# The delta rule's state stepped with the inverse multiplied out

## The chip, the cores and the metric

One core of a Trainium2 chip runs the whole program. The metric is device microseconds of one execution; the median of three runs of the kernel before is 2524.68 us. Engines: PE (TensorE matmul), DVE (VectorE), ACT (ScalarE), POOL (GpSimd), SP (SyncE, which issues most DMAs).

## The reference

A trunk of two layers on 256 tokens of width 2048. Layer 0 mixes by windowed attention and by a bidirectional gated delta rule, layer 1 by a Fourier transform; both have a SwiGLU network behind. The change concerns the delta rule of layer 0. For each of 8 heads and two directions it steps a 128x128 state `s` through the chunks, first those of the context, then those of the sequence:

```
sol = lax.linalg.triangular_solve(jnp.eye(DELTA_CHUNK, dtype=jnp.float32) + m, rhs, ...)
u, w = sol[..., :dv], sol[..., dv:]

def step(s, xs):
    u_i, w_i, attn_i, q_i, k_i, gl_i = xs
    v_new = u_i - jnp.einsum('bhcd,bhde->bhce', w_i, s)
    o_i = jnp.einsum('bhcd,bhde->bhce', q_i, s) + jnp.einsum('bhcs,bhse->bhce', attn_i, v_new)
    s = s * jnp.exp(gl_i)[..., None, None] + jnp.einsum('bhcd,bhce->bhde', k_i, v_new)
    return s, o_i
```

Everything is float32. With the inverse of the triangular matrix called Z, `v_new` is Z times (values minus scaled keys times state); it can be had as Z times that difference, or as Z times values minus (Z times scaled keys) times state.

## The kernel before

The kernel takes chunks of 128 tokens, so there are 4 chunks (2 of the context, 2 of the sequence), and 4 groups `g` of 2 heads. With 2 directions that gives 4 chains `q` to a group, and one PSUM tile of 128x512 holds a set of four 128x128 products, one a chain.

Work is written as Python generators. `gdn_a(g)` makes decays, the matrices and 16x16 blocks of the inverse (L729, L731 on DVE, with round trips through DRAM, `dz` and `dy`); `gdn_b(g)` completes the inverse `Z` and steps the state. Both are added to a list behind the projections of group `g`, and `step()` runs a piece of each whose time has come. That time is a count of PE work kept while the program is written (`clock`): after `yield 2` a piece waits for 2 x 1.2 us of counted matmul time, which the projections (tiles `acc`, three float32r products of split weights `whi`, `wlo`) fill. The tile framework then orders each engine's queue and sets the waits; every engine runs its queue in that order.

A step `t` of the chain (L845 to L899) before: keys times state into `pks` (PE); values plus scaled `pks` into `r` (tile `rw`, L854, DVE, four instructions); Z times `r` into `pw` (PE); `pw` scaled into `dv` (L865, ACT, four) and, where an output is due, `pw` as it is into `w` (L868, ACT, one wide); keys times `dv` into `pS` (PE); the state `St` from itself and `pS` (L883, or copies at L881 in the first step, DVE, four). In the last two steps query times state and attention times `w` make the output (L893 to L897). A `yield 2` parts the sets of products.

Beside the chain run, on DVE, the dots of `ada_dot` (L274, tile `araw`), each on 512 KB that SP loads; on ACT and POOL the splitting of weights (L197, L203); then attention (its probabilities in tiles `C2`, L1016, three buffers) and, at L1085, the gated output.

Of the kernel before, what the change touches and what calls it, by code (L numbers as in the profile page):

```python
# [11 lines left out]
F32R = mybir.dt.float32r  # L12
BF16 = mybir.dt.bfloat16
AF = mybir.ActivationFunctionType
ALU = mybir.AluOpType
AX = mybir.AxisListType

P = 128
# [7 lines left out]
HD = 128  # L26
# [45 lines left out]
def trunk(ctx: ExitStack, tc: tile.TileContext, a: dict, dbg=None, stop=None):  # L72
# [10 lines left out]
    def T(shape, tag, bufs, dt=F32):  # L83
        uid[0] += 1
        return sb.tile(list(shape), dt, tag=tag, bufs=bufs, name=f"{tag}_{uid[0]}")

    def C(shape, name, dt=F32):
        return sb.tile(list(shape), dt, tag=name, bufs=1, name=name)
# [10 lines left out]
    def ktok(shape, dt=F32):  # L99
        return T(shape, "KTOK", 1, dt)  # L100

    def vtok(shape, dt=F32):
        return T(shape, "VTOK", 1, dt)
# [7 lines left out]
    def qch(shape, dt=F32):  # L111
        return T(shape, "QCH", 2, dt)

    def e2(shape, dt=F32):
        return T(shape, "E2", 3, dt)
# [8 lines left out]
    def sm():  # L124
        uid[0] += 1
        return ps.tile([P, 512], F32, tag="sm", bufs=4, name=f"sm_{uid[0]}")
# [3 lines left out]
    def mm(out, l, r, start, stop):  # L130
        clock[0] += max(64, int(np.prod(r.shape[1:]))) * (4 if r.dtype == F32 else 1) / 2400.0
        nc.tensor.matmul(out, l, r, start=start, stop=stop)  # L132
# [4 lines left out]
    V = nc.vector  # L137
    S = nc.scalar
# [331 lines left out]
    for c in range(4):  # L470
# [3 lines left out]
                    in1=smallr[:, 0:1, :].to_broadcast([P, 4, 16]), op=ALU.add)  # L474
# [10 lines left out]
                           in1=ea.unsqueeze(1).to_broadcast([P, 4, 16]), op0=ALU.mult, op1=ALU.mult)  # L485
# [4 lines left out]
    egl = C([P, 4, 8, 2], "egl")  # L490
    pgc = sm()
    for d in range(2):
# [7 lines left out]
                           in1=gc.rearrange("p c h d -> p c (h d)"), op0=ALU.mult, op1=ALU.subtract)  # L500
# [121 lines left out]
    def bl(i, n=32):  # L622
        return slice(n * i, n * i + n)
# [118 lines left out]
    def gdn_b(g):  # L742
# [3 lines left out]
        K, Q, Z, Zv, A, Zc = (H[n] for n in ("K", "Q", "Z", "Zv", "A", "Zc"))  # L746
        ner, dvs, so1, so2 = H["sc"]
# [4 lines left out]
        if g == 0:  # L752
            Kt, Vt = H["Kt"], H["Vt"]
        else:
            Kt, Vt = ktok([P, 2, 4, HD]), vtok([P, 2, 4, HD])
# [86 lines left out]
        seqs = [(0, 1, 2, 3), (1, 0, 3, 2)]  # L842
        chains = [(hh * 2 + d, hh, d) for hh in range(2) for d in range(2)]
        St = T([P, 4, HD], "St", 1)
        for t in range(4):  # L845
            if t > 0:
                r = T([P, 4, HD], "rw", 2)
                pks = sm()
                for q, hh, d in chains:
                    c = seqs[d][t]  # L850
                    mm(pks[:, bl(q, P)], K[:, hh, bl(c, P)], St[:, q], True, True)
                for q, hh, d in chains:
                    c = seqs[d][t]
                    V.scalar_tensor_tensor(out=r[:, q], in0=pks[:, bl(q, P)], scalar=ner[:, c, hh, d:d + 1],  # L854
                                           in1=Vt[:, hh, c], op0=ALU.mult, op1=ALU.add)
                yield 2
            pw = sm()
            for q, hh, d in chains:
                c = seqs[d][t]
                mm(pw[:, bl(q, P)], Z[d][:, c, hh, :], r[:, q] if t > 0 else Vt[:, hh, c], True, True)  # L860
            if t < 3:
                dv = T([P, 4, HD], "rw", 2)
                for q, hh, d in chains:
                    c = seqs[d][t]
                    S.activation(dv[:, q], pw[:, bl(q, P)], AF.Copy, scale=dvs[:, c, hh, d:d + 1])  # L865
            if t >= 2:
                w = e2([P, 4, HD])
                S.activation(w.rearrange("p q f -> p (q f)"), pw, AF.Copy)  # L868
            yield 2
            if t >= 2:  # L870
                pqs = sm()
                for q, hh, d in chains:
                    mm(pqs[:, bl(q, P)], Q[:, hh, bl(seqs[d][t] - 2, P)], St[:, q], True, True)
            if t < 3:
                pS = sm()
                for q, hh, d in chains:
                    mm(pS[:, bl(q, P)], Kt[:, hh, seqs[d][t]], dv[:, q], True, True)
                for q, hh, d in chains:
                    c = seqs[d][t]
                    if t == 0:  # L880
                        V.tensor_copy(St[:, q], pS[:, bl(q, P)])  # L881
                    else:
                        V.scalar_tensor_tensor(out=St[:, q], in0=St[:, q], scalar=egl[:, c, 2 * g + hh, d:d + 1],  # L883
                                               in1=pS[:, bl(q, P)], op0=ALU.mult, op1=ALU.add)
            if t >= 2:
                paw = sm()
                for q, hh, d in chains:
                    mm(paw[:, bl(q, P)], A[:, d, hh, seqs[d][t] - 2], w[:, q], True, True)
                for q, hh, d in chains:
                    c = seqs[d][t] - 2  # L890
                    o = ogdn[c][:, 2 * g + hh]
                    if t == 2:
                        S.activation(o, pqs[:, bl(q, P)], AF.Copy, scale=so1[:, c, hh, d:d + 1])  # L893
                    else:
                        V.scalar_tensor_tensor(out=o, in0=pqs[:, bl(q, P)], scalar=so1[:, c, hh, d:d + 1], in1=o,
                                               op0=ALU.mult, op1=ALU.add)
                    V.scalar_tensor_tensor(out=o, in0=paw[:, bl(q, P)], scalar=so2[:, c, hh:hh + 1], in1=o,  # L897
                                           op0=ALU.mult, op1=ALU.add)
            yield 2  # L899


    def proj(warr, npair, lhs, tiles, kept=None, nkeep=0, last=0):
# [170 lines left out]
    for hf in range(2):  # L1073
# [9 lines left out]
        for t in range(2):  # L1083
            for h in range(4):
                V.scalar_tensor_tensor(out=zs[:, t, h], in0=ogdn[t][:, hf * 4 + h], scalar=rz[:, t * 4 + h:t * 4 + h + 1],  # L1085
                                       in1=zs[:, t, h], op0=ALU.mult, op1=ALU.mult)
        for hp in range(2):
            p = sm()
# [204 lines left out]
    for l in range(2):  # L1293
        if l == 1:
            plan_out(lambda n: a["w_four"][n], 8, NKF, 8)
        for j in range(NJ):
            for i in range(2):
                w = [a["w_gu"][l, j, i, q] for q in range(8)]
# [11 lines left out]
    def load_dft():  # L1310
        while f"hid{NJ - 2}" not in done:
            yield 1
        raws = [qch([P, 516]), qch([P, 512]), T([P, 512], "Zc", 1)]
        for i, src in enumerate((a["k_dft_d"], a["k_dft_l"][:, 0], a["k_dft_l"][:, 1])):
            nc.sync.dma_start(raws[i], src.rearrange("p k n -> p (k n)"))
        while f"hid{NJ - 1}" not in done:
            yield 1
        for f in (lambda: T([P, 516], "C2", 3, F32R), lambda: e2([P, 512], F32R), lambda: T([P, 512], "rw", 2, F32R)):
            dft.extend([f(), f()])
        for i in range(3):  # L1320
            yield DY
            split(dft[2 * i], dft[2 * i + 1], raws[i])
        yield DY
        dft.extend([c2([P, 512], F32R), T([P, 512], "Y64", 1, F32R)])
        for i in range(2):
            V.tensor_scalar_mul(dft[6 + i], dft[4 + i].bitcast(F32), -1.0)
# [191 lines left out]
```

## Time and profile before

| | |
|---|---|
| median of 3 runs | 2524.68 us (2523.31 to 2525.12) |
| the profiled execution | 2527.05 us |
| its span | 2525.2 us |
| first state step of group 0 on PE | 358.83 us |
| last state update of group 3 on DVE | 757.3 us |

The span runs from the first instruction to the last; the execution's time has 1.85 us around it. Terms of a sum are made against the profiled execution, which lies 2.37 us above the median of the runs. In rows of the trace a product of four chains shows as x8, two rows to each float32 product; x2 in the names of a queue's order counts equal rows in a row.

### The profile page before, as it was taken

What the parts mean: (1) busy time and instruction counts of PE and PEld (TensorE: products, weight loads), DVE (VectorE), ACT (ScalarE), POOL (GpSimd) and SP (SyncE); (2) the same over time, 40 slices, a digit from 0 to 9 for tenths busy, and PEclk for the clock granted to TensorE, in tenths of its full rate; (3) what the DMA queues carried; (4) which work ended last, traced back from release to release, by engine and by line L of the source; (5) the groups of instructions that cost most, each with busy time, mean ns of one, the idle gap of its engine ahead of it and who ended that gap; (6) DMA issues with size and microseconds to landing.
All of it is one profiled execution on the core that took longest, in us unless ns stands there. A gap on an engine that the chain in (4) does not pass through costs nothing.

```text
span 2525.2 us, 39613 instructions
## 1 busy us (share of the span) xinstructions
PE 2388.6 (95%) x14520; PEld 2022.8 (80%) x14520; DVE 1775.6 (70%) x3204; ACT 1274.6 (50%) x2298; POOL 332.5 (13%) x286
## 2 busy tenths in 40 slices
PE   7999888978799999999999999899999999999997
PEld 7998678867677788888888887697788888888886
DVE  4678788778657777877778788747666665555556
ACT  3337433544465654554445454646654554445455
POOL 1214434245431100000000000101100000000001
PEclk7999989989899999999999999999999999999998
DMA  6675778677837569999898998636577777666665
GB/s 252 244 288 197 236 224 272 208 245 253 263 130 237 197 228 316 312 312 317 319 318 312 315 322 308 211 102 217 191 235 242 232 237 234 193 191 189 191 201 191
DMA packets 218483, 611.04 MB, mean 242 GB/s; under 512 B 68905, under 2 KB 69913, under 8 KB 217521
## 3 DMA queue, kind: packets, MB, share of 16 engines
q1 hardware_dynamic: 168016, 581.59, 68.7%
q10 hardware_dynamic: 46528, 15.21, 2.6%
q0 software_dynamic: 3744, 11.71, 1.4%
q8 instruction: 114, 1.87, 0.3%
q14 instruction: 81, 0.66, 0.1%
HBM read 595.03 MB, written 13.40 MB: 241 GB/s over the span
## 4 chain that ended last, share of the span: by engine, by line
PE 70%; DVE 10%; DMA 6%; issue 3%; ACT 2%; POOL 1%; SPq 0%; ACTq 0%; DVEq 0%; POOLq 0%
PE acc L132 65%; PE sm L132 4%; DMA araw<-in_ada_d 4%; DVE araw L274 3%; DVE S L1153 1%; PE sm L1236 1%; DVE wlo L203 1%; POOL wlo L203 1%; ACT whi L197 1%; DVE C L513 1%; DVE T L729 0%; DMA T<-dy 0%; DVE T L731 0%; DMA T<-dz 0%; DMA raw<-in_w_dn 0%
## 5 line engine op out<-in xcount | busy, mean ns | idle before, releaser
L197 ACT ACTIVATE whi<-raw 128x512 fp32r<-128x512 f32 (+1 forms) x1306 | 817.9, 630 | 858.4 <-DVE wlo L203 489.1
L203 DVE TENSOR_TENSOR wlo<-raw,whi 128x512 fp32r<-128x512 f32 x1140 | 788.7, 699 | 469.8 <-ACT whi L197 468.1
L132 PE MATMUL acc<-whi,S 128*128 128x512 f32 x3312 | 1047.1, 394 | 8.1 <-ACT whi L197 3.7
L132 PEld LDWEIGHTS acc<-whi,S 128*128 128x128 f32 x3312 | 626.7, 190 | 139.5 <-ACT whi L197 4.5
L132 PE MATMUL acc<-wlo,S 128*128 128x512 f32 x1656 | 651.0, 393 | 3.8 <-DVE wlo L203 1.9
L274 DVE SCALAR_TENSOR_TENSOR araw<-araw,cb 128x1024 f32<-128x1024 f32 x320 | 415.6, 1300 | 66.9 <-DMA araw<-in_ada_d 66.3
L132 PEld LDWEIGHTS acc<-wlo,S 128*128 128x128 f32 x1656 | 314.1, 190 | 69.0 <-POOL wlo L203 2.9
L203 POOL TENSOR_TENSOR wlo<-raw,whi 128x512 fp32r<-128x512 f32 x166 | 245.7, 1493 | 445.2 <-ACT whi L197 429.3
L132 PE MATMUL acc<-S,whi 128*128 128x256 f32 x1152 | 235.1, 296 | 5.1 <-ACT whi L197 3.4
L132 PEld LDWEIGHTS acc<-S,whi 128*128 128x128 f32 x1152 | 193.3, 201 | 5.8 <-ACT whi L197 3.6
L132 PE MATMUL acc<-S,wlo 128*128 128x256 f32 x576 | 169.7, 296 | 2.0 <-POOL wlo L203 2.0
L1113 POOL DMA_DIRECT2D drow<-K x4 | 2.0, 508 | 1273.9 <-DVE K L1111 1273.9
L132 PE MATMUL acc<-whi,ZT 128*128 128x512 f32 x384 | 122.1, 392 | 0.0
L132 PEld LDWEIGHTS acc<-S,wlo 128*128 128x128 f32 x576 | 115.9, 201 | 3.5 <-POOL wlo L203 2.6
L132 PE MATMUL acc<-whi,KCH 128*128 128x512 f32 x320 | 110.7, 402 | 1.1 <-ACT whi L197 1.1
L132 PE MATMUL acc<-whi,A 128*128 128x512 f32 x312 | 106.0, 395 | 0.0
L132 PE MATMUL acc<-whi,T 128*128 128x512 f32 x296 | 99.5, 392 | 0.0
L132 PEld LDWEIGHTS acc<-whi,ZT 128*128 128x128 f32 x384 | 72.1, 188 | 15.3
L132 PE MATMUL acc<-wlo,KCH 128*128 128x512 f32 x192 | 78.0, 406 | 4.3 <-DVE wlo L203 4.1
L132 PE MATMUL acc<-wlo,ZT 128*128 128x512 f32 x192 | 75.6, 394 | 0.2 <-POOL wlo L203 0.2
L132 PEld LDWEIGHTS acc<-whi,KCH 128*128 128x128 f32 x320 | 62.2, 195 | 15.2 <-ACT whi L197 1.5
L132 PE MATMUL acc<-wlo,T 128*128 128x512 f32 x176 | 68.8, 391 | 0.0
(437 smaller groups left out, 2829.2 us busy)
## 6 DMA issues: line engine op xcount, KB each, us to landing
raw<-in_w_gu SPq DMA_DIRECT2D x347, 512.0 KB, 4.4
araw<-in_ada_d SPq DMA_DIRECT2D x320, 512.0 KB, 4.8
raw<-in_w_dn SPq DMA_DIRECT2D x179, 512.0 KB, 4.4
raw<-in_w_att SPq DMA_DIRECT2D x40, 512.0 KB, 4.4
raw<-in_w_gdn SPq DMA_DIRECT2D x34, 512.0 KB, 4.8
raw<-in_w_out SPq DMA_DIRECT2D x30, 512.0 KB, 3.7
ZT<-in_ada_s SPq DMA_DIRECT2D x24, 512.0 KB, 3.7
raw<-in_w_four SPq DMA_DIRECT2D x21, 512.0 KB, 3.7
```

What stands on the lines that cost most here:

```text
L132: nc.tensor.matmul(out, l, r, start=start, stop=stop)
L197: S.activation(hi[:, :w], raw[:, c:c + w], AF.Copy)
L203: eng.tensor_sub(lo[:, :w], raw[:, c:c + w], hi[:, :w].bitcast(F32))
L274: V.scalar_tensor_tensor(out=junk, in0=w, scalar=1.0, in1=rows, op0=ALU.mult, op1=ALU.mult, accum_out=dst)
L513: V.scalar_tensor_tensor(out=ca[:, :, lo:hi], in0=pv[:, :, lo + o:hi + o], scalar=wconv[:, blk, j:j + 1], in1=ca[:, :, lo:hi], op0=ALU.mul ...
L1113: nc.gpsimd.dma_start(drow.rearrange("h k p -> (h k) p"), gt)
L1153: V.scalar_tensor_tensor(out=x[:, t, sl], in0=y[:, t, sl], scalar=r, in1=x[:, t, sl], op0=ALU.mult, op1=ALU.add)
L1236: nc.tensor.transpose(p[:, i * P:(i + 1) * P], hv[t][:, i * P:(i + 1) * P], ident)
```

## The change

The step is taken apart differently. `weights(t + 1)`, a step ahead, scales the keys (L854 of the new file, ACT, four, tile `C2`), multiplies them by Z (PE) and copies the product to `wt` (L864, DVE, one wide copy into `rw`). Z times values then goes to `pw`, and `wt` times state is added to it in the accumulator. `pw` is evacuated once, wide (L878, ACT); the scale that was on `dv` goes on a second scaled copy of the keys, `kd` (ACT, four, `C2`), which also is made ahead. The first state is one wide copy (L891); L894 answers to L883. The pauses are 1.5 in place of 2, two of them a step, `rw` has three buffers in place of two, and the evacuated `w` lives there and no longer in `E2`.

```diff
--- before.py
+++ after.py
@@ -842,31 +842,43 @@
         seqs = [(0, 1, 2, 3), (1, 0, 3, 2)]
         chains = [(hh * 2 + d, hh, d) for hh in range(2) for d in range(2)]
         St = T([P, 4, HD], "St", 1)
+
+        def flat(v):
+            return v.rearrange("p q f -> p (q f)")
+
+        def scaled(tag, by, t):
+
+            kk = T([P, 4, HD], tag, 3)
+            for q, hh, d in chains:
+                c = seqs[d][t]
+                S.activation(kk[:, q], Kt[:, hh, c], AF.Copy, scale=by[:, c, hh, d:d + 1])
+            return kk
+
+        def weights(t):
+
+            kn = scaled("C2", ner, t)
+            p = sm()
+            for q, hh, d in chains:
+                mm(p[:, bl(q, P)], kn[:, q], Z[d][:, seqs[d][t], hh, :], True, True)
+            wt = T([P, 4, HD], "rw", 3)
+            V.tensor_copy(flat(wt), p)
+            return wt
+
+        kd = scaled("C2", dvs, 0)
+        wt = None
         for t in range(4):
-            if t > 0:
-                r = T([P, 4, HD], "rw", 2)
-                pks = sm()
-                for q, hh, d in chains:
-                    c = seqs[d][t]
-                    mm(pks[:, bl(q, P)], K[:, hh, bl(c, P)], St[:, q], True, True)
-                for q, hh, d in chains:
-                    c = seqs[d][t]
-                    V.scalar_tensor_tensor(out=r[:, q], in0=pks[:, bl(q, P)], scalar=ner[:, c, hh, d:d + 1],
-                                           in1=Vt[:, hh, c], op0=ALU.mult, op1=ALU.add)
-                yield 2
             pw = sm()
             for q, hh, d in chains:
-                c = seqs[d][t]
-                mm(pw[:, bl(q, P)], Z[d][:, c, hh, :], r[:, q] if t > 0 else Vt[:, hh, c], True, True)
+                mm(pw[:, bl(q, P)], Z[d][:, seqs[d][t], hh, :], Vt[:, hh, seqs[d][t]], q == 0, t == 0 and q == 3)
+            if t > 0:
+                yield 1.5
+                for q, hh, d in chains:
+                    mm(pw[:, bl(q, P)], wt[:, q], St[:, q], False, q == 3)
+            w = T([P, 4, HD], "rw", 3)
+            S.activation(flat(w), pw, AF.Copy)
             if t < 3:
-                dv = T([P, 4, HD], "rw", 2)
-                for q, hh, d in chains:
-                    c = seqs[d][t]
-                    S.activation(dv[:, q], pw[:, bl(q, P)], AF.Copy, scale=dvs[:, c, hh, d:d + 1])
-            if t >= 2:
-                w = e2([P, 4, HD])
-                S.activation(w.rearrange("p q f -> p (q f)"), pw, AF.Copy)
-            yield 2
+                wt = weights(t + 1)
+            yield 1.5
             if t >= 2:
                 pqs = sm()
                 for q, hh, d in chains:
@@ -874,14 +886,16 @@
             if t < 3:
                 pS = sm()
                 for q, hh, d in chains:
-                    mm(pS[:, bl(q, P)], Kt[:, hh, seqs[d][t]], dv[:, q], True, True)
-                for q, hh, d in chains:
-                    c = seqs[d][t]
-                    if t == 0:
-                        V.tensor_copy(St[:, q], pS[:, bl(q, P)])
-                    else:
-                        V.scalar_tensor_tensor(out=St[:, q], in0=St[:, q], scalar=egl[:, c, 2 * g + hh, d:d + 1],
+                    mm(pS[:, bl(q, P)], kd[:, q], w[:, q], True, True)
+                if t == 0:
+                    V.tensor_copy(flat(St), pS)
+                else:
+                    for q, hh, d in chains:
+                        V.scalar_tensor_tensor(out=St[:, q], in0=St[:, q],
+                                               scalar=egl[:, seqs[d][t], 2 * g + hh, d:d + 1],
                                                in1=pS[:, bl(q, P)], op0=ALU.mult, op1=ALU.add)
+                if t < 2:
+                    kd = scaled("C2", dvs, t + 1)
             if t >= 2:
                 paw = sm()
                 for q, hh, d in chains:
@@ -896,7 +910,7 @@
                                                op0=ALU.mult, op1=ALU.add)
                     V.scalar_tensor_tensor(out=o, in0=paw[:, bl(q, P)], scalar=so2[:, c, hh:hh + 1], in1=o,
                                            op0=ALU.mult, op1=ALU.add)
-            yield 2
+        yield 2
 
 
     def proj(warr, npair, lhs, tiles, kept=None, nkeep=0, last=0):
@@ -1315,7 +1329,7 @@
             nc.sync.dma_start(raws[i], src.rearrange("p k n -> p (k n)"))
         while f"hid{NJ - 1}" not in done:
             yield 1
-        for f in (lambda: T([P, 516], "C2", 3, F32R), lambda: e2([P, 512], F32R), lambda: T([P, 512], "rw", 2, F32R)):
+        for f in (lambda: T([P, 516], "C2", 3, F32R), lambda: e2([P, 512], F32R), lambda: T([P, 512], "rw", 3, F32R)):
             dft.extend([f(), f()])
         for i in range(3):
             yield DY
```

The order of the queues moves with it. Three places follow, in the program's names (numbers of buffers stay where the program prints them).

PE, group 0: from the product that makes the first state (`rw` by keys) to the product that reads it. Before:

```order
L132 MATMUL sm_3778<-rw_3736,KTOK_1851 128x128 x4
L132 MATMUL acc_3696<-S_75_425,whi_3569 128x256
L132 MATMUL acc_3696<-S_75_425,wlo_3570 128x256
L132 MATMUL acc_3696<-S_76_426,whi_3569 128x256
...
L132 MATMUL acc_3696<-S_74_424,whi_3699 128x256
L132 MATMUL sm_3834<-St_3730,KCH_1850 128x128 x4
```

Now:

```order
L132 MATMUL sm_3786<-rw_3741,C_524_3731 128x128 x4
L132 MATMUL sm_3797<-VTOK_1852,ZT_2454 128x128
L132 MATMUL sm_3797<-VTOK_1852,ZT_2455 128x128
...
L132 MATMUL acc_3696<-S_75_425,whi_3569 128x256
...
L132 MATMUL acc_3696<-S_74_424,whi_3569 128x256
L132 MATMUL sm_3797<-St_3730,rw_3753 128x128 x4
L132 MATMUL sm_3843<-ZT_2454,C_537_3838 128x128
```

Between the two stood 24 projection products of 256 columns; now there stand the set Z by values and 18 of them, and the set Z by scaled keys follows at once.

DVE, group 1: ahead of the state's third version before, and between its first and second version now (`T` is the block inverse of group 2, `araw` a dot). Before:

```order
L731 TENSOR_TENSOR T_723_5321<-T_723_5321 128x12x4
L729 TENSOR_TENSOR T_723_5321<-T_723_5321 128x55
L513 SCALAR_TENSOR_TENSOR C_750_5510<-acc_5251,wconv,C_750_5510 128x2x254
L731 TENSOR_TENSOR T_723_5321<-T_723_5321 128x11x5
L513 SCALAR_TENSOR_TENSOR C_750_5510<-acc_5251,wconv,C_750_5510 128x2x255
L883 SCALAR_TENSOR_TENSOR St_5095<-St_5095,egl,sm_5487 128x128 x4
```

Now:

```order
L891 COPY St_4911<-sm_4957 128x512
L274 SCALAR_TENSOR_TENSOR araw_6014,adaacc_5678<-araw_6014,cb 128x1024
L274 SCALAR_TENSOR_TENSOR araw_6072,adaacc_5678<-araw_6072,cb 128x1024
L864 COPY rw_5022<-sm_5017 128x512
L572 COPY lens<-sm_5024 128x2
L274 SCALAR_TENSOR_TENSOR araw_6108,adaacc_5678<-araw_6108,cb 128x1024
L274 SCALAR_TENSOR_TENSOR araw_6197,adaacc_5678<-araw_6197,cb 128x1024
L894 SCALAR_TENSOR_TENSOR St_4911<-St_4911,egl,sm_5046 128x128 x4
```

The block inverse of group 2 no longer stands among group 1's states; four dots stand between two of them.

PE, group 3, which runs among the attention heads (transposes of their probabilities at L1020, L1034 in the new file): from the first state's product to its reader. Before:

```order
L132 MATMUL sm_7958<-rw_7904,KTOK_7066 128x128 x4
L132 MATMUL acc_7827<-whi_7992,S_74_424 128x512
L132 MATMUL acc_7828<-whi_7992,S_73_423 128x512
...
L132 MATMUL acc_7827<-whi_8168,S_73_423 128x512
L1020 MATMUL sm_7979<-ident,C_1145_7923 128x128 x4
L132 MATMUL sm_8000<-St_7898,KCH_6243 128x128 x4
```

Now:

```order
L132 MATMUL sm_7981<-rw_7935,C_1148_7925 128x128 x4
L132 MATMUL sm_7992<-VTOK_7182,ZT_6563 128x128
L132 MATMUL sm_7992<-VTOK_7182,ZT_6564 128x128
...
L1034 MATMUL sm_7997<-ident,C_1146_7915 128x128 x4
L132 MATMUL sm_7992<-St_7924,rw_7947 128x128 x4
L132 MATMUL sm_8013<-E_1167_8002,ZT_7134 128x128 x4
```

Seventeen projection products of 512 columns and the transposes stood between them; now there are one set and the transposes.

## Rows read from the trace of the kernel before

**Rows 1.** The page, busy us by engine, share of the span, instructions
```profile
PE 2388.6 (95%) x14520; PEld 2022.8 (80%) x14520; DVE 1775.6 (70%) x3204; ACT 1274.6 (50%) x2298; POOL 332.5 (13%) x286
```

**Rows 2.** Two stretches: busy us, instructions by engine, PEclk, DMA
```profile
core 0: us, PE busy (x) PEld busy (x) DVE busy (x) ACT busy (x) POOL busy (x), PEclk, DMA share, GB/s
358.00:796.00 438.00, 375.06 (x4011) 324.51 (x4009) 332.46 (x751) 213.30 (x449) 173.18 (x133) 0.93 0.72 230
796.00:2525.20 1729.20, 1693.51 (x7687) 1396.93 (x7687) 1189.36 (x1934) 904.09 (x1536) 55.47 (x47) 0.99 0.74 245
```

**Rows 3.** PE's waits, 358 to 796 us: us in total, times, longest
```profile
PE sm L132 <- DVE St L883: 12.2, 6, 4.6
...
PE sm L1020 <- ACT C L1016: 6.7, 4, 3.2
PE sm L132 <- DMA T<-dy: 6.6, 1, 6.6
PE sm L132 <- DVE St L881: 4.7, 1, 4.7
...
PE sm L1091 <- DVE ZT L1085: 1.3, 1, 1.3
```

**Rows 4.** PE in order of time, group 0's chain; bracket: idle before, releaser
```profile
358.83 1.05 PE L132 MATMUL sm<-VTOK,ZT 128*128 128x128 f32 x8
359.64 0.36 PE L132 MATMUL acc<-S,whi 128*128 128x256 f32 x1
...
362.60 1.05 PE L132 MATMUL sm<-rw,KTOK 128*128 128x128 f32 x8
...
371.21 2.05 PE L132 MATMUL sm<-St,KCH 128*128 128x128 f32 x8 [4.69 <-DVE St L881]
...
393.92 1.05 PE L132 MATMUL sm<-St,QCH 128*128 128x128 f32 x8
394.81 1.06 PE L132 MATMUL sm<-rw,KTOK 128*128 128x128 f32 x8
```

**Rows 5.** PE in order of time, the other long waits for a state
```profile
401.77 1.84 PE L132 MATMUL sm<-St,KCH 128*128 128x128 f32 x8 [2.14 <-DVE St L883]
...
512.58 2.07 PE L132 MATMUL sm<-St,KCH 128*128 128x128 f32 x8 [4.57 <-DVE St L883]
...
627.98 2.07 PE L132 MATMUL sm<-St,KCH 128*128 128x128 f32 x8 [3.57 <-DVE St L883]
```

**Rows 6.** Single lines: duration ns min/median/max, first and last start, forms
```profile
L854 DVE SCALAR_TENSOR_TENSOR rw<-sm,gsc,VTOK x48: 335/342/351, 374.8 to 763.1; 128x128 f32<-128x128 f32 x48
L881 DVE COPY St<-sm x16: 271/278/293, 370.9 to 734.4; 128x128 f32<-128x128 f32 x16
L766 DVE COPY E<-sm x4: 682/686/691, 326.7 to 667.9; 128x512 f32<-128x512 f32 x4
L865 ACT ACTIVATE rw<-sm,gsc x48: 347/368/411, 359.9 to 755.6; 128x128 f32<-128x128 f32 x48
L868 ACT ACTIVATE E<-sm x8: 578/598/615, 393.7 to 764.8; 128x512 f32<-128x512 f32 x8
L1016 ACT ACTIVATE C<-C,col x16: 705/722/724, 660.7 to 764.2; 128x512 f32<-128x512 f32 x16
L509 ACT ACTIVATE C<-acc,wconv x21: 453/672/710, 191.5 to 554.3; 128x512 f32<-128x512 f32 x15, 128x256 f32<-128x256 f32 x6
```

**Rows 7.** DVE in order of time, group 1
```profile
507.70 0.18 DVE L729 TENSOR_TENSOR T<-T 128x15 f32<-128x15 f32 x1 [2.87 <-DMA T<-dz]
...
512.19 1.11 DVE L883 SCALAR_TENSOR_TENSOR St<-St,egl,sm 128x128 f32<-128x128 f32 x4
```

**Rows 8.** L274: 358 to 796 us (busy, mean ns, idle before), then by stretch
```profile
L274 DVE SCALAR_TENSOR_TENSOR araw<-araw,cb 128x1024 f32<-128x1024 f32 x90 | 127.1, 1414 | 45.5 <-DMA araw<-in_ada_d 45.0
...
440.00:450.00 10.00, 4.93 (x8) 0.68 0.73 241
...
460.00:470.00 10.00, 3.68 (x6) 1.00 0.71 223
```

## The prediction

> **What bounds the kernel now.** I began with the page's busy table: PE is busy for 95% of the span and every other engine for less [rows 1]. That is a mean over stages, so the second view was busy time by stretch [rows 2]. I chose the cuts by where the two programs differ: on PE's queue they are alike up to the first state step at 358 us, and behind the gated output (L1085, at 780 us) they differ in a few dozen rows out of thousands. So only the middle stretch, 358 to 796 us, can change, and there PE is busy 375.06 us of 438, DVE 332.46, ACT 213.30. PE leads, but 62.9 us of its time is idle.
>
> The third view is what ended PE's waits in that stretch [rows 3]. The longest total belongs to the state `St`: 12.2 us behind L883 and 4.7 us behind L881, 16.9 us in 7 waits. All are the first product of a step, keys times state [rows 4, 5]. No wait of PE is behind `rw` written by DVE (L854): the round trip through DVE that the change takes out is covered by projection work today. What makes `St` late is seen on DVE. It runs its queue in order, and between two states stand the dots of L274, which wait for their own DMA (90 of them, 45.5 us idle before them [rows 8]), or, in group 1, a row of L729 that waits for the block inverse's round trip through DRAM [rows 7].
>
> **The change, part by part.** A group is two heads in two directions, so each step has four products to a set.
>
> *PE.* Per group the sets go from 14 to 17: three sets keys-times-state become three sets `wt`-times-state, and three sets inverse-times-keys are added. From the start of one set of four to the next is 394.81 - 393.92 = 0.89 us [rows 4]; 3 x 4 groups x 0.89 = **+10.7 us** of PE. Values times inverse, first overwriting and then accumulated, costs PE the same as before. I take it whole, since in the stretch PE is the busiest engine and its waits are behind other engines' late work.
>
> *DVE.* Out per group: 12 scaled additions into `rw` at 342 ns and 4 copies into `St` at 278 ns, 5.2 us. In: 4 copies of 128x512 out of PSUM, taken at the 686 ns of L766, the same shape and source, 2.7 us [rows 6]. So -2.5 us a group, -10 us in all. Little of it is on the path: per step 4 x 342 becomes 686 ns, 0.68 less, in front of the next state; where a state keeps PE waiting that shortens the wait. Of 12 reads of a state 7 wait. In group 0's first step the state itself becomes one copy that PE must wait for whole, 686 in place of a first quarter at 278 (+0.4). I take 5 x 0.68 - 0.4 = **-3.0 us**.
>
> *ACT.* Out per group: 12 scaled evacuations of 368 ns and 2 wide ones of 598. In: 4 wide ones and 24 scaled copies of keys from SBUF [rows 6]. The trace has no 128x128 copy from SBUF with a column scale; bounds are 368 ns (same size, from PSUM) and 722 ns (L1016, from SBUF, 512 columns). The nearer is the first, plus what SBUF costs more: L1016 722 against L509 672, a median in which 6 of 21 are half as wide, so some 0.04 to 0.05; about 410 ns. That is +6.6 us a group, some 27 us in all. The sum gets nothing for it: keys and scales are there long before, in groups 0 and 1 ACT's order has nearly all of a step's scaled keys ahead of the evacuation they are used with, and ACT is busy for half the stretch. If that cover goes it is the third rival below. The Trainium skill (VectorE: DVE Perf Modes, The TRN2 errata) states a fixed cost for each small operation, 224 cycles and one a column at 1.2 GHz from SBUF, an estimate of 293 ns; the row for 128 columns, 368, lies above it. By its figure ACT would gain 15 us in place of 27; the sum stays.
>
> *Distance on PE between a state and its reader.* Before: 24 projection instructions of 256 columns, 362.60 - 359.64 = 2.96 us [rows 4]. After, by the order of groups 0 and 1: one set (0.89) and 18 such, 0.89 + 2.2 = 3.1 us. So a late state is covered as well, or as badly, as now, and I leave the waits of groups 0 and 2 where they are.
>
> *Group 1.* Its longest wait, 4.57 us, stems from the inverse of group 2 running beside it [rows 5, 7]. In the new order that piece stands behind the chain: the wait goes, and with it the slow set after it, 2.07 against 1.05 us. That is -5.6. But four dots now stand between two of its states. The trace gives 3 to 4 dots in 10 us there (each with a read of the accumulator, so x6 and x8) [rows 8], so four need 10 to 13.3 us, while PE is back at the state after 4 x 0.89 + 2 x 2.2 = 8.0: +2.0 to +5.4, taken as 3.7. **-1.9 us**.
>
> *Group 3.* Its order has only one set and four transposes between product and reader (0.89 us and a little) where projection rows stood. DVE needs 1.11 us for four states [rows 7] and may be in a reduction; no dots are left there. Three reads of 0 to 0.7 us: **+1.0**.
>
> *Tail.* Group 3 ends 36 projection instructions of 256 columns (4.4 us) earlier, and PE's first wait for the gated output, 1.3 us [rows 3], should go: **-1.3**.
>
> Sum: 10.7 - 3.0 - 1.9 + 1.0 - 1.3 = **+5.5 us**, on the profiled execution's 2527.05 us 2532.6. That execution lies 2.4 us above the median of the runs, 2524.68, so against that median 2530.2 us.
>
> **Rivals.** *Faster: the waits for the state go.* A chain without `rw` on DVE needs half the trips, and if the states then arrive in time, the 16.9 us go, and with them the slow sets behind the four long waits, which took 1.84 to 2.07 us against 1.05 [rows 4, 5], some 4 us. 10.7 - 16.9 - 4.0 - 1.3 = -11.5: 2513.2 us. It decides once more than half of that 20.9 us is saved. For it: group 1's longest wait has a cause that moves away. Against it: the dots stay in front of the states, and the distance on PE hardly grows. The slow sets show PE's clock at its lower level after an idle time. The Trainium skill (TensorE: Matmul & The Clock Gate, HAM oscillation) says that each such idle time is paid twice, by the wait and by the slow restart, and the trace agrees.
>
> *No change: the added sets fill idle time.* PE idles 62.9 us in the stretch, and dots and round trips through DRAM (6.6 us behind `dy` [rows 3]) keep their own pace; if PE merely arrives later at waits that end at the same moment, half or more of the 10.7 is absorbed: 2524 to 2527 us, 2525.5. For it: DVE's 45.5 us behind DMA. Against: most PE idle time is not in the steps that grow.
>
> *Slower by more: the C2 buffers.* Scaled keys live in `C2`, three buffers shared with the convolutions and with attention's probabilities. A key tile waits there for a whole step. PE waits 6.7 us today for those probabilities (L1016) [rows 3]. If the chain of group 3, which now runs among the attention heads, doubles that, it is 5.5 + 6.7 = +12.2: 2536.9 us. It decides if ACT's allocations wait for a key tile's last product.
>
> That the change doesn't do what it says is excluded by the order: the sets stand there as described.
>
> **How the numbers follow.** Forecast 0.37, faster rival 0.27, absorbed 0.22, buffers 0.14. What a measurement can tell here is 0.2%, 5.0 us, so the line is at 2529.7. The forecast's own terms move by some 3 us (the dots of group 1 alone by 1.7), so about 0.08 of its 0.37 falls within: same 0.30, slower 0.29 + 0.14 = 0.43, faster 0.27. For 8 in 10 the range goes from the faster rival's value, 2513, to above the buffers' with the dots at their upper bound, 2536.9 + 1.7, and some 2 more for reads of group 3 at theirs: 2541. Some 0.1 is left out at each end.
>
> **What would show it.** Right: PE busy in the middle stretch up by some 10 us and DVE down by as much; `sm<-St,rw` with waits behind L894 of 10 to 17 us in total, one of them in group 1 behind dots; no wait behind the new copies (L864). Wrong: waits behind `St` under 8 us in total (faster), waits for L1030's probabilities or for L854's keys over 10 us (buffers), or PE idle time down by about 10 us with the end unmoved (absorbed).

## The result and the profile after

The changed kernel takes 2544.41 us (median of 4 runs, 2536.95 to 2547.74); the kernel before, run beside it, 2523.99. The ratio is 1.0079, interval 1.0054 to 1.0104: by the medians 20.4 us slower where 5.5 were forecast, and above the range. The profiled execution took 2547.74 us, its span is 2545.9 at a mean granted clock of 0.966 (before 0.970).

The page's busy line after, which answers to [rows 1]:

```profile
PE 2409.7 (95%) x14616; PEld 2039.9 (80%) x14616; DVE 1767.7 (69%) x3156; ACT 1297.4 (51%) x2356; POOL 333.7 (13%) x286
```

PE has the 96 added instructions of 12 sets (two rows to a float32 product) and is busy 21.1 us longer. Its idle time is the same: 2545.9 - 2409.7 = 136.2, before 2525.2 - 2388.6 = 136.6. Added work would be 10.7 of those 21.1. The rest, 10.4, is about what the lower mean clock makes of the old work: 2388.6 us at 0.970 become 9.9 us more at 0.966, an estimate.

Busy time by stretch, columns as in [rows 2]. The gated output ends 20 us later, so the middle stretch is cut at 816:

```profile
358.00:816.00 458.00, 393.12 (x4087) 339.05 (x4086) 322.69 (x702) 234.09 (x503) 173.43 (x133) 0.91 0.69 219
816.00:2545.90 1729.90, 1694.46 (x7696) 1397.64 (x7694) 1189.13 (x1933) 904.88 (x1538) 56.30 (x47) 0.99 0.74 245
```

Behind it nothing changed (1729.9 us, before 1729.2). In it PE is up by 18.1 us, DVE down by 9.8 and ACT up by 20.8.

PE's waits in that stretch, which answer to [rows 3]:

```profile
PE sm L132 <- DVE St L894: 12.3, 4, 4.4
PE acc L132 <- ACT whi L197: 8.9, 5, 3.2
...
PE sm L132 <- DVE E L766: 6.1, 1, 6.1
PE sm L132 <- DMA QCH<-dq: 5.3, 1, 5.3
PE acc L132 <- POOL wlo L203: 4.3, 7, 1.4
...
PE acc L132 <- DVE wlo L203: 2.3, 1, 2.3
...
PE sm L132 <- DVE St L891: 1.4, 1, 1.4
PE sm L132 <- DVE rw L864: 1.1, 1, 1.1
PE sm L1034 <- ACT C L1030: 0.9, 3, 0.4
```

The state still keeps PE waiting, 13.7 us against 16.9. The new copies (L864) hardly do, and the probabilities cost less than before (0.9 for 6.7). What has grown is `acc` behind `whi` and `wlo`: the projection itself waits for its split weights, 15.5 us in all for 6.8 before. The long waits for a state are now in groups 1 and 2, PE in order of time, as in [rows 5]:

```profile
474.81 2.08 PE L132 MATMUL sm<-St,rw 128*128 128x128 f32 x8 [3.87 <-DVE St L894]
...
648.30 2.08 PE L132 MATMUL sm<-St,rw 128*128 128x128 f32 x8 [4.39 <-DVE St L894]
```

Group 1's is behind a dot that waited for its DMA, DVE in order of time:

```profile
473.26 1.23 DVE L274 SCALAR_TENSOR_TENSOR araw<-araw,cb 128x1024 f32<-128x1024 f32 x1 [3.50 <-DMA araw<-in_ada_d]
...
474.41 1.12 DVE L894 SCALAR_TENSOR_TENSOR St<-St,egl,sm 128x128 f32<-128x128 f32 x4
```

Single lines after, columns as in [rows 6]:

```profile
L854 ACT ACTIVATE C<-KTOK,gsc x96: 384/388/417, 357.6 to 771.7; 128x128 f32<-128x128 f32 x96
...
L864 DVE COPY rw<-sm x12: 678/686/692, 364.6 to 772.8; 128x512 f32<-128x512 f32 x12
```

The wide copy is the 686 ns taken; a scaled key copy takes 388 ns for the 410 estimated. The Trainium skill (ScalarE: Activation LUTs, What ACT_TABLE_LOAD costs) gives 280 ns and 0.833 a column for one operand by pointer, an estimate of 387 ns, and the trace agrees.

Two pieces of the stretch show best how it has changed, 540 to 600 and 660 to 720 us. Before:

```profile
540.00:600.00 60.00, 51.05 (x832) 42.09 (x833) 46.78 (x87) 36.08 (x75) 35.34 (x24) 0.91 0.80 263
...
660.00:720.00 60.00, 46.54 (x772) 34.65 (x771) 38.30 (x91) 30.91 (x73) 22.75 (x18) 0.94 0.65 222
```

After:

```profile
540.00:600.00 60.00, 43.63 (x547) 33.61 (x546) 40.60 (x85) 25.89 (x45) 34.08 (x26) 0.83 0.78 225
...
660.00:720.00 60.00, 45.84 (x560) 34.95 (x559) 42.93 (x101) 22.92 (x49) 27.91 (x21) 0.83 0.79 250
```

From 540 to 600 us PE is busy 7.4 us less, at a mean clock of 0.83 for 0.91; from 660 to 720 the clock is 0.83 again, where it was 0.94. These are not the only pieces that differ: from 420 to 480 us the clock is 0.81 for 0.92, and from 480 to 540, where it is 0.94 for 0.91, PE is busy 3.9 us more. What left the piece from 540 to 600 us is seen on PE in order of time, by the first and one of the last products of group 2's block inverse (`Zc`, then 64x64). Before:

```profile
544.54 0.85 PE L132 MATMUL sm<-T,Zc 32*32 32x32 f32 x44 [6.63 <-DMA T<-dy]
...
581.56 1.15 PE L132 MATMUL sm<-ZT,E 64*64 64x64 f32 x32
```

After:

```profile
587.66 1.93 PE L132 MATMUL sm<-T,Zc 32*32 32x32 f32 x128
...
621.99 1.15 PE L132 MATMUL sm<-ZT,E 64*64 64x64 f32 x32
```

The inverse comes 43 us later. In PE's order it begins after 2088 projection products (counted in 256 columns) before and after 2280 now; group 1's after 1629 and 1518, group 3's after 2610 and 2650. By the code that follows from the pauses: short ones end a chain sooner and so start the next group's inverse and chain sooner (1518), and a chain that has run already adds nothing to the counted time in which group 2's inverse is prepared, so that takes more projection. Between 540 and 587 us the projection then has no products of an inverse beside it.

### The profile page after: what moved, and what is told of

Its sections match the earlier page's. It is cut to its first block, busy times and chain, and to the rows that moved or that the text cites. A ratio compares the mean times of both kernels' runs of the same rounds, so it can differ in the third digit from the quotient of the medians.

```text
span 2545.9 us, 39834 instructions
## 1 busy us (share of the span) xinstructions
PE 2409.7 (95%) x14616; PEld 2039.9 (80%) x14616; DVE 1767.7 (69%) x3156; ACT 1297.4 (51%) x2356; POOL 333.7 (13%) x286
## 4 chain that ended last, share of the span: by engine, by line
PE 70%; DVE 10%; DMA 6%; issue 3%; ACT 2%; POOL 1%; ACTq 0%; SPq 0%; DVEq 0%; POOLq 0%
PE acc L132 64%; PE sm L132 5%; DMA araw<-in_ada_d 4%; DVE araw L274 3%; DVE T L729 1%; DVE S L1167 1%; PE sm L1250 1%; DVE T L731 1%; DVE C L513 1%; POOL wlo L203 1%; DMA dz<-Zc 1%; DVE wlo L203 1%; ACT whi L197 0%; PE sm L1034 0%; DMA T<-dz 0%
## 5 line engine op out<-in xcount | busy, mean ns | idle before, releaser
L274 DVE SCALAR_TENSOR_TENSOR araw<-araw,cb 128x1024 f32<-128x1024 f32 x320 | 413.1, 1292 | 86.9 <-DMA araw<-in_ada_d 86.6
```

The costliest lines, as they stand in the source:

```text
L274: V.scalar_tensor_tensor(out=junk, in0=w, scalar=1.0, in1=rows, op0=ALU.mult, op1=ALU.mult, accum_out=dst)
```

## The experiments

The theories: the **place** (the pauses, 12.5 for 22 units a group, move the following groups' inverses), the **work** (three added sets a group), **C2** (key tiles held there), **ACT** (scaled copies). Each ratio is to the kernel before, run on the same chip; 1.0000 there is 2518.6 to 2520.6 us, so 0.1% is 2.5 us.

### The pauses alone

```diff
-                yield 2          (before the products with the inverse)
+                yield 1.5
-            yield 2              (before the state's products)
+            yield 1.5
-            yield 2              (at the end of each step)
+        yield 2                  (once, behind the last)
```

> The kernel before, with only the pauses of the changed kernel in the chain (1.5 instead of 2, and one closing pause for a group instead of one a step): 12.5 us of paced work for a group in place of 22, the arithmetic and the instructions untouched. If the loss of 20 us beyond the work comes from the chain being bunched (a2 and b2 later, projections without chain work beside them, which outrun the weights): 2524 + 7 to 10 = 2531 to 2534. If it comes from the three added sets and from the key tiles held in C2: no change, 2521 to 2527. If shorter pauses expose the four-operation steps of the old chain: more waits behind L869/L881/L883 and also 2530 or more, but then PE's waits behind St in 358 to 796 rise from 23 us to over 30.

Ratio **1.0062** (1.0046 to 1.0079). The kernel before, with no arithmetic changed, loses 16 us. PE's waits, 358 to 830 us:

```profile
PE acc L132 <- ACT whi L197: 6.9, 5, 2.4
PE acc L132 <- POOL wlo L203: 6.5, 6, 1.7
PE acc L132 <- DVE wlo L203: 4.6, 1, 4.6
PE sm L132 <- DVE St L883: 3.6, 2, 2.5
```

The waits for the state fell, to 10.6 in all with L881, from the 16.9 of [rows 3] (the 23 of the expectation is in no such row); those for weights rose to 18.0, where the kernel before has 6.8.

### The three sets alone

```diff
+                px = sm()
+                for q, hh, d in chains:
+                    mm(px[:, bl(q, P)], Kt[:, hh, seqs[d][t]], Z[d][:, seqs[d][t + 1], hh, :], True, True)
                 dv = T([P, 4, HD], "rw", 2)
```

> The kernel before plus three sets of four products a group (the inverse times the unscaled keys of the next step, 128 columns each, into a PSUM tile that nobody reads), at the place where the changed kernel has them. It leaves the DVE, ACT and tile traffic of the kernel before as it is. If TensorE's added work is paid whole: 12 sets x 0.89 = 10.7 us, 2532 to 2537. If it fills waits that were there: 2522 to 2528. If it costs clock too, as the stretch of the changed kernel shows (0.91 for 0.93): over 2537.

Ratio **1.0009** (0.9996 to 1.0022): -1 to +5.5 us for work that takes 10.7. The page's busy line:

```profile
PE 2395.0 (95%) x14616; PEld 2029.2 (81%) x14616; DVE 1776.6 (71%) x3204; ACT 1276.7 (51%) x2299; POOL 333.7 (13%) x286
```

PE is busy 6.4 us longer than in [rows 1] and idle 17.7 less (2513.9 - 2395.0 = 118.9, for 136.6). Its waits for the state are 6.8 us in place of 16.9:

```profile
PE sm L132 <- DVE St L886: 3.7, 5, 2.0
PE sm L132 <- DVE St L884: 3.1, 1, 3.1
```

So half or more of the added work is not paid for, by the ratio. That it fills waits, PE coming later to states that come no later, is what the two profiles say; how much of the 17.7 is that can't be told from them, since this profile is of the fastest of its 12 runs (2515.68 us) and that of the kernel before lies above its median. Two near copies of the kernel before, further down, have waits for the state of 11.3 (`e8_scaled_keys_alone`) and 12.9 us (`e14_dy_off_sp_before`).

### Keys out of C2, then the old pauses

```diff
-        kd = scaled("C2", dvs, 0)
+        kd = scaled("Y64", dvs, 0)
```

> The changed kernel with the keys scaled by the decay (kd) in the tile of Y64, which is free while the chain runs, instead of in C2, whose three buffers the evacuations of the projections and of q, k, v also take. If C2 delays those and through them a2 and b2: 2530 to 2538, with the tiles of Q of group 2 back near the place that they had before. If C2 is not what costs: 2541 to 2548, as the changed kernel.

Ratio **1.0107** (1.0090 to 1.0123), no better than the changed kernel's 1.0079. The decayed keys `kd` in C2 are not what costs; the keys scaled for the weights stayed there. With the three pauses of 2 a step put back as well:

> As the run with kd in its own tile, and with the three pauses of 2 a step that the kernel before has (22 us of paced work for a group's chain, in place of 12.5). If bunching costs: 8 us or more under the run with the short pauses, 2525 to 2535. If the added work alone sets the time, as the sum had it: 2528 to 2535 only if the run with the short pauses is there too. If neither pauses nor C2 matter: 2541 to 2548. If the change's spared DVE work is worth more than the added sets once the order is that of before: under 2524.

Ratio **1.0050** (1.0032 to 1.0068): the pauses are 14 us of this kernel too. What is left is 12.6 us. The waits for `St` are gone from PE's list; two on ACT's writes stand in their place:

```profile
PE sm L132 <- ACT C L854: 8.1, 5, 4.4
...
PE sm L132 <- ACT rw L878: 5.8, 3, 3.6
```

### What is left: ACT, the accumulator, the scaled keys

All on the kernel with kd in its own tile and the old pauses, but for the last. Without any scaling of keys:

```diff
-                mm(p[:, bl(q, P)], kn[:, q], Z[d][:, seqs[d][t], hh, :], True, True)
+                mm(p[:, bl(q, P)], Kt[:, hh, seqs[d][t]], Z[d][:, seqs[d][t], hh, :], True, True)
-                    mm(pS[:, bl(q, P)], kd[:, q], w[:, q], True, True)
+                    mm(pS[:, bl(q, P)], Kt[:, hh, seqs[d][t]], w[:, q], True, True)
```

> The run with kd in its own tile and the old pauses, and without the 28 scaled copies of keys a group (both products take the unscaled keys, so neither decay nor write strength enters the products; the output is not the reference's). It takes 28 x 388 ns = 10.9 us of ACT work from each group. If what is left of the loss (ratio 1.005, 12 us) is ACT, whose copies the trace now names where St was named (C L854 8.1 us, rw L878 5.8 us): ratio 0.996 to 1.001. If it is TensorE's added work or the order: 1.003 to 1.007.

Ratio **1.0023** (1.0010 to 1.0036), short of the 1.001 that ACT as the cause asked for and below the 1.003 that the other causes did: it decides for neither. The copies taken away are 24 a group (x96 in all), not 28. With the accumulator opened behind the pause:

```diff
+            if t > 0:
+                yield 2
             pw = sm()
...
-                yield 2
```

> The run with kd in its own tile and the old pauses, with the inverse times values issued behind the pause, next to the products that add to it, so that one of the four PSUM tiles that all small work shares is not held over the pause. If holding it is what costs: ratio 1.000 to 1.002. If ACT's copies cost: 1.004 to 1.007, as without this edit.

Ratio **1.0029** (1.0015 to 1.0043). With the weights' keys scaled on DVE:

```diff
-                S.activation(kk[:, q], Kt[:, hh, c], AF.Copy, scale=by[:, c, hh, d:d + 1])
+                V.tensor_scalar_mul(kk[:, q], Kt[:, hh, c], by[:, c, hh, d:d + 1])
```

> The run with kd in its own tile and the old pauses, with the 12 copies a group scaled for the weights made on DVE instead of ACT (12 x 388 = 4.7 us a group from ACT, to an engine that the change has given back 10 us in all). If ACT's queue is what costs: ratio 1.001 to 1.003, the waits behind L854 half or less of 8.1 us. If it is the order or the PSUM tiles: 1.004 to 1.007. If DVE is as tight as ACT: 1.006 or more, with waits behind DVE for the copies.

Ratio **1.0034** (1.0019 to 1.0050). PE's waits for these copies now stand behind DVE and are longer, 16.2 us for the 8.1 behind ACT, and the kernel is no slower for it. Both of these edits together, run in the next series:

> The changed kernel with kd in its own tile, the old pauses, the accumulator opened behind the pause, and the weights' keys scaled on DVE: both edits that took the ratio from 1.0050 to 1.0029 and 1.0034 together. If they are separate costs that add up: 1.000 to 1.0015. If both only took one and the same wait, or were scatter: 1.002 to 1.004.

Ratio **1.0023** (1.0012 to 1.0035). They don't add up, and taking all 24 copies a group away gives no more. These four lie in each other's intervals, and their 1.0023 to 1.0034 against 1.0050 is at the edge of what can be told. Besides, in all four the order moved as well: group 2's inverse begins after 2124 projection products, with the old pauses alone after 2088. Neither ACT nor the PSUM tile is shown as a cost, nor excluded as one; part of the 1.0050 may be scatter.

The kernel before with kd and one wide evacuation, nothing else of the change:

```diff
-                    S.activation(dv[:, q], pw[:, bl(q, P)], AF.Copy, scale=dvs[:, c, hh, d:d + 1])
+            w = T([P, 4, HD], "rw", 2)
+            S.activation(w.rearrange("p q f -> p (q f)"), pw, AF.Copy)
```

> The kernel before with one part of the change: keys scaled ahead (kd, in C2), so that one evacuation of 512 columns serves the state's product and the output, in place of four scaled ones and, in two steps of four, a fifth. Pauses, the right side on DVE and the products are those of before. ACT does the same number of copies, but 12 x 4 of them beside the chain and not in it. If ACT's copies beside the chain cost as much as in it: ratio 0.999 to 1.002. If the step's length is what counts: 0.994 to 0.998. If C2 held over the pauses costs: over 1.003.

Ratio **0.9992** (0.9978 to 1.0005): no difference. A shorter step brings nothing here, nor do the decayed keys in C2 cost anything.

### The place held by a closing pause

Short pauses inside the chain as in the change, and the time that they save given back behind the last step, first on the kernel before, then on the changed one with kd in its own tile:

```diff
-        yield 2
+        yield 11.5
```

> The kernel before with the short pauses inside the chain, as in the run short pauses (ratio 1.0062), but with a closing pause of 11.5 in place of 2, so that a group still takes 22 and the next group's block inverse stands where it stood (after some 1620, 2130 and 2600 projection products of 256 columns; with the short pauses it was 1518, 2280 and 2664). If the cost of short pauses is that shift, which leaves the projection between 540 and 600 us without chain work and waiting for weights: ratio 0.999 to 1.002, waits of the projection for whi and wlo back from 18 us to under 9. If it is the steps standing closer: 1.004 to 1.008.

Ratio **1.0017** (1.0007 to 1.0027), from 1.0062.

> The changed kernel with kd in its own tile (ratio 1.0107) and a closing pause of 11.5 in place of 2; the steps of the chain stay as close as the change has them. Shift alone: ratio 1.004 to 1.006, as with the old pauses inside (1.0050). Close steps: 1.008 to 1.012.

Ratio **1.0027** (1.0015 to 1.0040), from 1.0107: below the range expected even of the place alone. In the order group 2's inverse begins after 2132 and 2109 projection products. The steps stand as close as the change has them, so their distance is at most what is left, 4 us on the kernel before. The two runs of the changed kernel differ in that pause alone. PE's first products of group 2's inverse and two stretches, with the old place lost:

```profile
582.54 1.72 PE L132 MATMUL sm<-T,Zc 32*32 32x32 f32 x128 [4.41 <-DMA T<-dy]
```

```profile
540.00:600.00 60.00, 43.93 (x601) 34.58 (x600) 38.29 (x85) 25.50 (x44) 28.91 (x23) 0.83 0.68 214
...
660.00:720.00 60.00, 47.38 (x718) 35.82 (x715) 40.34 (x100) 27.30 (x61) 23.28 (x19) 0.86 0.75 233
```

and with it held:

```profile
543.58 1.29 PE L132 MATMUL sm<-T,Zc 32*32 32x32 f32 x128
```

```profile
540.00:600.00 60.00, 51.76 (x861) 43.05 (x860) 44.85 (x79) 41.73 (x93) 29.47 (x20) 0.94 0.76 257
...
660.00:720.00 60.00, 50.75 (x835) 38.63 (x834) 39.69 (x93) 34.91 (x85) 22.34 (x18) 0.97 0.69 234
```

The spans are 2542.7 and 2523.3, and PE's busy time by the page 2399.3 and 2390.2. Of the 19.4 us, 9.1 are the same PE instructions at a lower clock, and 10.3 are idle (143.4 and 133.1). That share of clock fits the mean clocks, 0.972 and 0.976. In both stretches shown, PE is idle longer with the place lost, by 7.8 and 3.4 us, and its clock is lower. But the loss isn't theirs alone: the rest of the 358 to 830 us differs by as much either way, most of all from 420 to 480 us, where PE is idle 8.8 us less with the place lost. There, place lost and then held:

```profile
420.00:480.00 60.00, 53.31 (x833) 51.54 (x822) 45.69 (x85) 33.46 (x75) 21.93 (x15) 0.89 0.75 250
```

```profile
420.00:480.00 60.00, 44.48 (x887) 41.15 (x886) 47.46 (x86) 37.36 (x76) 18.75 (x14) 0.94 0.69 234
```

Nor is half of it clock in every case: on the kernel before, short pauses with and without the closing pause have spans of 2521.4 and 2530.0, and of those 8.6 us 6.9 are idle (134.2 and 141.1). What PE waited for from 540 to 600 us in the changed kernel, place lost:

```profile
PE acc L132 <- ACT whi L197: 5.9, 3, 3.8
PE sm L132 <- DMA T<-dy: 4.4, 1, 4.4
PE acc L132 <- POOL wlo L203: 3.2, 3, 1.7
PE sm L132 <- issue: 2.4, 1, 2.4
```

With the place held no wait there is for weights. Over the whole stretch to 816 us, though, the waits for weights are about alike (17.8 and 18.2 us), and in the run on the kernel before they are 14.3, not under 9: that expectation failed. The place doesn't do away with waits for weights; PE's idle time in all is what fell. The closing pause moves all that follows a group's chain, the next chain and the next inverse alike, so which of these pieces costs by its place isn't separated.

### Longer, and a little shorter

```diff
-            yield 2              (all three of a step, the kernel before)
+            yield 2.5
```

> The kernel before with pauses of 2.5 in place of 2 in the chain, nothing else: 27.5 us of paced work for a group. It asks whether the place of the chain has an optimum at the old value. Shorter is dearer by 0.6%, so longer may gain if cover is short everywhere: 0.996 to 0.999; if the groups then run late into attention and the gated output: 1.002 or more.

Ratio **1.0092** (1.0074 to 1.0109): dearer than shortening by 9.5 units. PE's list has `DVE ZT L1085` with 8.1 us and 1.3 before: the last group runs into the gated output.

```diff
-            yield 2              (end of each step, the kernel before)
+            if t < 3:
+                yield 2
```

> The kernel before without the last pause of a group, so 20 in place of 22; every step keeps its distance. In the order the block inverse of group 2 then stands behind 2216 projection products of 256 columns instead of 2088 to 2130, group 3's behind 2678 instead of 2610 (2280 and 2664 in the changed kernel). If the place is what costs: 1.003 to 1.006. If it is the length of the chain by the measure of its change (2 of the 9.5 that cost 0.6%): 1.000 to 1.002.

Ratio **1.0042** (1.0029 to 1.0056). Two units cost two thirds of what 9.5 cost, and every step keeps its distance: the place counts, not the length. In the order group 2's inverse moves by two thirds as well, to 2216 products from 2088, where the short pauses have it at 2280; group 3's moves too. Its stretch from 540 to 600 us:

```profile
540.00:600.00 60.00, 48.39 (x767) 37.39 (x766) 39.91 (x70) 25.26 (x51) 30.98 (x25) 0.84 0.73 231
```

### SP behind the block inverse

In the changed kernel SP, which loads the weights (L187), stands between them for its half of the inverse's write to `dy` (L739). SP's issues in order of time, then PE's two longest waits for `whi`:

```profile
562.83 2.83 SPq L187 DMA_DIRECT2D raw<-in_w_att  x2
570.99 1.31 SPq L739 DMA_DIRECT2D dy<-T  x2
572.40 3.84 SPq L187 DMA_DIRECT2D raw<-in_w_att  x2
```

```profile
573.36 0.79 PE L132 MATMUL acc<-whi,S 128*128 128x512 f32 x1 [3.17 <-ACT whi L197]
...
584.29 1.22 PE L132 MATMUL acc<-whi,S 128*128 128x512 f32 x2 [3.11 <-ACT whi L197]
```

ACT, which splits the weights and issues the other half of that write, stands there too. Its issues and splits in the same time:

```profile
570.99 1.59 ACTq L739 DMA_DIRECT2D dy<-T  x2
572.68 1.15 ACT L197 ACTIVATE whi<-raw 128x512 fp32r<-128x512 f32 x2 [7.67 <-issue]
...
577.90 5.61 ACTq L555 DMA_DIRECT2D dVt<-E  x1
583.61 2.19 ACT L197 ACTIVATE whi<-raw 128x512 fp32r<-128x512 f32 x4 [5.22 <-issue]
```

PE's first wait ends with a split that ACT could begin only behind its own half of the write to `dy`, the second with one behind the 5.61 us in which ACT issues another write (`dVt`). Neither split waited for weights still to land (`issue` means that the profile shows no wait of the instruction itself). So the two waits are not shown to come from SP, and the edit below, which takes SP out, puts its half on ACT:

```diff
-                (S, nc.sync)[s].dma_start(dy[i][:, :, :, sl, sl].rearrange("d e b r c -> (d e b) r c"), Y2[bl(s, 64), i])
+                S.dma_start(dy[i][:, :, :, sl, sl].rearrange("d e b r c -> (d e b) r c"), Y2[bl(s, 64), i])
```

> The changed kernel with the block inverse's write to dy (L739) issued by ACT alone, where SP issued half of it with the projections' weights behind it. If SP standing there is what starves PE between 540 and 600 us: the waits behind whi there fall from 8.9 us to under 4, and with the clock that they cost the ratio goes from 1.0079 to 1.003 to 1.005. If the projection without small work beside it outruns its weights anyway: the waits stay or move to the next buffer, ratio 1.006 to 1.010.

Ratio **1.0133** (1.0113 to 1.0153), worse. ACT now issues the whole write and stands for it; ACT's waits from 540 to 600 us:

```profile
ACT whi L197 <- DMA dy<-T: 11.0, 1, 11.0
```

PE's waits behind `whi` from 540 to 600 us are 7.8 us for 8.9, not under 4 as expected of SP as the cause; from 358 to 830 us they rise to 15.1, from 8.9, by one of 6.5 us at 678 us. The same edit on the kernel before:

> The kernel before with the same edit, the control: its write to dy falls where the projection has small work beside it, so nothing should change, 0.998 to 1.002. If SP standing costs in every place: under 0.998, and then the run with the changed kernel says nothing of the place.

Ratio **0.9997** (0.9986 to 1.0009). There too ACT's splits wait for that write, 12.2 us in two waits. So more of the write on ACT's queue costs where the inverse has the changed kernel's place (1.0133 for 1.0079, though measured on different chips) and nothing where it has the old one. Of SP standing there it shows nothing, and whether the changed kernel would gain from a queue that neither loads nor splits weights wasn't tried.

## Why the prediction was wrong

**The step that failed is the one on group 1**, "in the new order that piece stands behind the chain: the wait goes", with its -5.6. The order showed that the block inverse of group 2 moves, and the working asked only what it leaves. Nothing was charged for where it arrives, or for what else moves with it. Giving the places back is worth 11 us (1.0062 to 1.0017 on the kernel before) to 20 us (1.0107 to 1.0027 on the changed one with `kd` in its own tile), more than any term of the sum. Inside group 1's chain the term was not far off: the wait behind the inverse went, and one of 3.87 us behind a dot that had waited 3.50 us for its own DMA took its place (3.7 were taken), with a slow set of 2.08 us after it as before; -0.7 us where the sum has -1.9. The pauses stand in the diff and had no term of their own; they came in only through the order, as the distance between a state and its reader. No rival held this either: the slower one was C2.

**PE, +10.7**: too large as a price. The sets alone cost -1 to +5.5 us. The rival "absorbed" was right for them. The reason given against it ("most PE idle time is not in the steps that grow") did not hold: in that profile the waits for the state, which are in those steps, are 10 us less.

**DVE, -3.0**: DVE's busy time fell by 9.8 us as worked out, and the waits for the state by 3.2; but no kernel with the change was faster for it.

**ACT, 0**: not settled. Without any scaled copy the kernel takes 1.0023, with them 1.0023 to 1.0050, so up to 7 us may be theirs or none. The third rival's sign, waits over 10 us for the probabilities or for the scaled keys, did not come (0.9 and 0.7 us).

**Group 3 and tail**, +1.0 and -1.3: too small to be seen beside the rest. The longest waits for a state are in groups 1 and 2, and PE no longer waits for the gated output; a wait of 5.3 us for attention's queries (`dq`) is new, and the kernel with the sets alone has it too.

With the place held the change costs 0.27%, 6.7 us, where the sum said 5.5. That is no proof of the sum, since its largest term is not what the sets alone cost. What the remaining 6.7 consist of is open: the sets are up to 5.5 of it, and no edit to ACT or PSUM took it below 1.0023. Of the signs named ahead, DVE down, `St` waits of 10 to 17 us and next to none for the copies came true, and PE's busy time rose by 18 us where some 10 were named; they didn't speak of the places, where the loss was. Shown is that the places of what follows a chain cost, by pauses alone. By which piece and which wait they cost is open; in the pair of the changed kernel half of it is clock, in that of the kernel before a fifth. The changed kernel itself, with `kd` in C2, was not run with the closing pause.

No version with a part of the change beats the kernel before: keys scaled ahead alone come nearest, and the interval holds 1.

## What to carry to other kernels

Where background work is interleaved by counted time, a pause is also a clock for everything that starts when the piece ends: before pricing the instructions of a changed piece, list where each later piece begins in the old and the new order, and hold those places (a closing pause of the time saved) when testing the arithmetic. Where main work loses its small companions, look at the supply of its operands, at every queue that stands between them (the one that converts them as well as the one that loads them), and at the granted clock; but compare the whole stretch, since what one piece loses another may gain. Work added ahead of waits may be nearly free, and work spared where it is covered may bring as little.

## What was not expected of the hardware

Runs of one kernel differ by their clock. In 34 runs of the kernel before on one chip the mean granted clock went from 0.969 to 0.976 and the time from 2532 to 2514 us; a straight line through them gives 1.6 us for 0.001 and leaves about half of their scatter. Kernels that lose the place also run at a lower mean clock (0.9697 and 0.9692 where the kernel before beside them has 0.9730), by that line 5 to 6 of their 16 and 27 us. That fits a PE whose idle time costs more than its length, and the kernel with the three sets alone, which has a mean of 0.974; which of clock and time brings the other about, the runs don't show.
